# Low halves of the mixing projections' weights: the negated high half plus an accumulating transfer, in place of a subtraction

## The chip, the core and the metric

The kernel runs on one core of a Trainium2 chip. The metric is device time in microseconds (us) of one execution, smaller is better. Five engines work beside each other, each through its own instructions in order, tied together by semaphores: PE (TensorE, matmuls), DVE (VectorE), ACT (ScalarE), POOL (GpSimd) and SP (SyncE, which here only issues transfers). A queue of a transfer belongs to the engine that issues it; the data is moved by 16 DMA engines.

## The reference, cut to what matters

One encoder layer over 512 tokens of width 1024, all in float32:

```python
h = h + 0.5 * swiglu(rms_norm(h, ffn1_norm[l]), ...)
u = rms_norm(h, mix_norm[l]) @ w_in[l]            # 1024 -> q 512 | k 128 | v 128 | pool channels 512
q, k, v, pc = jnp.split(u, ...)
a = window_attention(rope(q), rope(k), v, sink_logits[l])
p = multiscale_pool(pc, pool_w[l], pool_scale[l])
h = h + jnp.concatenate([a, p], axis=-1) @ w_out[l]
h = h + 0.5 * swiglu(rms_norm(h, ffn2_norm[l]), ...)
return rms_norm(h, final_norm)
```

## The kernel before

**Precision.** Each large product is made of three matmuls in the format fp32r. An operand is split in a high half (a rounded copy) and a low half (the operand less its high half); `mm3` (L113) adds high by high, high by low and low by high in one PSUM bank. For activations the halves are called `xh`, `xl`, `yh`, `yl` and so on. For weights they are `wh` and `wl`, and in a projection of this kernel L114 is `wh` by `yh`, L115 `wh` by `yl`, and L116 `wl` by `yh`. So the third matmul of the first step of a weight half is the first that needs `wl`.

**Weight stream.** All weights come through one stream. A unit is 1 MB (128 x 2048), loaded by SP into one of two `raw` buffers; `split_next` (L78) takes one half of a unit (128 x 1024) at a time: ACT copies it to `wh` (L97), and DVE, or for a few halves POOL, subtracts `raw - wh` into `wl` (L98). There are four `wh` and four `wl` buffers, and `weights` (L103) splits up to two halves ahead of the one in use. A `raw` buffer is loaded anew when all that read it are done, and `wh` and `wl` are written anew when PE is done with them.

**The mixing part.** `w_in` is five units, ten halves of 24 matmuls each, in this order: k, v (woven into each other), pool channel group 3, query 0, group 2, queries 1, 2, 3, groups 1 and 0. I count them as first to tenth half. `w_out` is four units, eight halves. In before, POOL subtracts the first, second, fourth and sixth half of `w_in` and the first, fourth and seventh of `w_out` (the tables `WIN_POOL`, `WOUT_POOL`), and DVE the others.

**Work around it.** After the pool channel group 3 the sums of the norm are made (`norm_sums`) and spread (`norm_spread`, L198 on PE, L199 on ACT). Then DVE turns each product into what attention needs: for a query the rotation (`rope`, L357 to L360, with `u` as result), a scaled copy by ACT (L390), and the low half (L391) into `qq`. `pool_means` (L410) scales a group on DVE into `uu` (L418), sums windows on POOL (L425, L431, `dd` at L434), and goes back to DVE (L437) and on. Scores are two matmuls (L518, L519), a masked sum on DVE (L520) and an exponential on ACT (L523); POOL divides (L530); transposes (L547), copies (L551, L552) and products (L562, L563) follow. The order in which each engine takes its instructions is fixed when the program is built, by a scheduler that goes by estimated times, so an edit can move instructions that it doesn't touch.

Of the kernel before, what the change touches and what calls it, by code (L numbers as in the profile page):

```python
# [8 lines left out]
F32 = mybir.dt.float32  # L9
F32R = mybir.dt.float32r  # L10
AF = mybir.ActivationFunctionType
ALU = mybir.AluOpType
# [14 lines left out]
AFTER = 11  # L27
EARLY = 12
LAG = 4
WIN_POOL = (0, 1, 3, 5)  # L30
WOUT_POOL = (0, 3, 6)
POOL_W = (2, 4, 8, 16)
PAD = 8

# [2 lines left out]
def encoder_layer(ctx: ExitStack, tc: tile.TileContext, xT, w1h, w1gu, w1d, win, wout, w2h, w2gu, w2d,  # L37
                  gains, gfin, sinks, poolw, pscale, cosT, sinT, edges, out):
    nc = tc.nc
# [15 lines left out]
    units = [(w1h, i) for i in range(KD // 2)] + [(w1gu, i) for i in range(NF - F0)]  # L55
# [7 lines left out]
    def load(i, between=None):  # L63
        src, j = units[i]
        n = src.shape[-1] // 2
        if i in early:
            return early.pop(i)
        raw = wts.tile([P, 2048], F32, name="raw", tag="raw", bufs=2)
        if i == 0:
            for q in range(4):  # L70
                between(q)
                queue = nc.sync if q else nc.scalar
                queue.dma_start(raw[:, q * n // 2:(q + 1) * n // 2], src[j][:, q * n // 2:(q + 1) * n // 2])
        else:
            nc.sync.dma_start(raw[:, :2 * n], src[j])
        return raw, n

    def split_next():  # L78

        i, half = stream["asked"] // 2, stream["asked"] % 2  # L80
        if i == len(units):
            return
        if half == 0 and i:
            stream["raw"] = load(i)
        raw, n = stream["raw"]
        src = raw[:, half * n:(half + 1) * n]
        spare = stream.get("spare")
        if spare:
            wh, wl = spare.pop(0)
        else:  # L90
            wh = wts.tile([P, 1024], F32R, name="wh", tag="wh", bufs=4)[:, :n]
            wl = wts.tile([P, 1024], F32R, name="wl", tag="wl", bufs=4)[:, :n]
        m = n // 2 if stream["asked"] == 0 else n
        on_pool = WIN_POOL if units[i][0] is win else WOUT_POOL if units[i][0] is wout else ()
        sub = nc.gpsimd if 2 * units[i][1] + half in on_pool else nc.vector
        for c in range(0, n, m):
            nc.scalar.copy(wh[:, c:c + m], src[:, c:c + m])  # L97
            sub.tensor_tensor(wl[:, c:c + m], src[:, c:c + m], wh[:, c:c + m].bitcast(F32),  # L98
                              op=ALU.subtract)
        stream["asked"] += 1  # L100
        stream["ready"].append((wh, wl))

    def weights(ahead=2):  # L103
        while len(stream["ready"]) <= ahead and stream["asked"] < 2 * len(units):
            split_next()
        return stream["ready"].pop(0)
# [686 lines left out]
```

## Time and profile before

| What | us |
|---|---|
| median of 3 runs (lowest, highest) | 891.06 (889.69, 891.23) |
| the profiled execution's own time | 891.37 |
| its span | 889.6 |
| PE busy in the span | 872.2 (98%) |
| DVE busy | 408.4 (46%) |
| ACT busy | 309.9 (35%) |
| POOL busy | 311.8 (35%) |
| mean granted TensorE clock | 0.994 |

The span is the profiled stretch from the first instruction to the last; some 1.8 us lie around it. Matmul ends are modelled, so the distance from one matmul's start to the next one's (0.23 us for 512 columns at full clock) tells more than a duration of 0.39 us. The page's chain of work that ended last goes through PE for 92% and through DVE for 4%.

### The profile page before, as it was taken

The numbers are of one execution on the slowest core, as the hardware profiler recorded it, in microseconds if no ns is written. First come the engines' busy times: TensorE is split into PE (matmuls) and PEld (weight loads), VectorE is DVE, ScalarE is ACT, GpSimd is POOL, SyncE is SP. The second block draws the span as 40 slices with busy tenths as digits, with TensorE's granted clock in tenths as the row PEclk, the third lists the DMA queues.
The fourth block names the chain that finished last, engine by engine and source line by source line (L and its number), as shares of the span: only waits on it lengthen the run. The fifth ranks groups of instructions, "written<-read, shape, count | busy, mean of one in ns | idle before, by whom it ended". The sixth has DMA issues, their size and how long they took to land.

```text
span 889.6 us, 9675 instructions
## 1 busy us (share of the span) xinstructions
PE 872.2 (98%) x3918; PEld 719.3 (81%) x3918; DVE 408.4 (46%) x516; ACT 309.9 (35%) x454; POOL 311.8 (35%) x255
## 2 busy tenths in 40 slices
PE   8999999999999999999789999999999999999996
PEld 7888888888888888887668888888888888888885
DVE  6444444444432221669887643444444444322225
ACT  7353222333321111543666532533323322211223
POOL 5186444444420001855542220763444444200004
PEclk9999999999999999999999999999999999999998
DMA  6422222222222222221211123122222222332202
GB/s 237 156 81 95 95 97 98 102 106 101 104 102 95 95 95 95 84 95 50 97 44 36 61 93 125 66 95 95 94 95 95 95 94 95 127 104 104 105 11 94
DMA packets 14683, 84.79 MB, mean 95 GB/s; under 512 B 1824, under 2 KB 2352, under 8 KB 5808
## 3 DMA queue, kind: packets, MB, share of 16 engines
q1 hardware_dynamic: 13104, 81.60, 25.8%
q10 hardware_dynamic: 1440, 2.57, 0.9%
q8 instruction: 30, 0.49, 0.2%
q14 instruction: 13, 0.11, 0.0%
q0 software_dynamic: 96, 0.02, 0.0%
HBM read 82.08 MB, written 2.10 MB: 95 GB/s over the span
## 4 chain that ended last, share of the span: by engine, by line
PE 92%; DVE 4%; ACT 1%; POOL 1%; issue 1%; DMA 0%; DVEq 0%; POOLq 0%; ACTq 0%
PE ps L114 29%; PE ps L115 29%; PE ps L116 29%; DVE qq L391 1%; PE ps L547 1%; DVE wl L98 1%; PE ps L563 1%; PE ps L562 1%; DVE rtmp L359 1%; DMA small<-in_gains 0%; PE ps L655 0%; DVE u L360 0%; PE ps L226 0%; PE ps L228 0%; PE ps L198 0%
## 5 line engine op out<-in xcount | busy, mean ns | idle before, releaser
L98 DVE TENSOR_TENSOR wl<-raw,wh 128x1024 fp32r<-128x1024 f32 (+2 forms) x146 | 215.6, 1478 | 206.2 <-ACT wh L97 197.7
L97 ACT CAST wh<-raw 128x1024 fp32r<-128x1024 f32 (+2 forms) x153 | 156.3, 1024 | 415.1 <-PE ps L115 339.3
L114 PE MATMUL ps<-zh,wh 128*128 128x512 f32 x346 | 135.5, 392 | 0.0
L115 PE MATMUL ps<-zl,wh 128*128 128x512 f32 x346 | 135.1, 390 | 0.0
L116 PE MATMUL ps<-xh,wl 128*128 128x512 f32 x346 | 135.0, 391 | 0.0
L114 PE MATMUL ps<-xh,wh 128*128 128x512 f32 x346 | 134.8, 390 | 0.0
L116 PE MATMUL ps<-zh,wl 128*128 128x512 f32 x346 | 134.8, 390 | 0.0
L115 PE MATMUL ps<-xl,wh 128*128 128x512 f32 x346 | 134.6, 389 | 0.0
L208 POOL TENSOR_TENSOR t<-t,t 128x512 f32<-128x512 f32 x44 | 77.7, 1769 | 146.0 <-ACT t L207 146.0
L210 POOL TENSOR_TENSOR t<-t,rstd 128x512 f32<-128x512 f32 x44 | 61.2, 1394 | 99.3 <-DVE t L209 99.3
L209 DVE TENSOR_TENSOR t<-ps,t 128x512 f32<-128x512 f32 x44 | 30.4, 691 | 120.2 <-PE ps L116 108.2
L114 PEld LDWEIGHTS ps<-xh,wh 128*128 128x128 f32 x346 | 64.9, 188 | 13.9 <-ACT wh L97 0.2
L116 PEld LDWEIGHTS ps<-zh,wl 128*128 128x128 f32 x346 | 64.9, 188 | 13.9 <-issue 0.2
L116 PEld LDWEIGHTS ps<-xh,wl 128*128 128x128 f32 x346 | 64.9, 188 | 14.0 <-issue 0.2
L115 PEld LDWEIGHTS ps<-zl,wh 128*128 128x128 f32 x346 | 65.0, 188 | 13.4 <-issue 0.2
L115 PEld LDWEIGHTS ps<-xl,wh 128*128 128x128 f32 x346 | 65.0, 188 | 13.4
L114 PEld LDWEIGHTS ps<-zh,wh 128*128 128x128 f32 x346 | 65.0, 188 | 13.2
L206 DVE TENSOR_TENSOR t<-ps,rstd 128x512 f32<-128x512 f32 x44 | 30.2, 691 | 92.3 <-PE ps L116 75.9
L114 PE MATMUL ps<-a1h,wh 128*128 128x512 f32 x176 | 68.5, 389 | 0.0
L115 PE MATMUL ps<-a1l,wh 128*128 128x512 f32 x176 | 68.5, 389 | 0.0
L116 PE MATMUL ps<-a1h,wl 128*128 128x512 f32 x176 | 68.5, 389 | 0.0
L98 POOL TENSOR_TENSOR wl<-raw,wh 128x1024 fp32r<-128x1024 f32 x7 | 16.8, 2396 | 117.3 <-ACT wh L97 114.3
(189 smaller groups left out, 1270.2 us busy)
## 6 DMA issues: line engine op xcount, KB each, us to landing
raw<-in_w1gu SPq DMA_DIRECT2D x19, 1024.0 KB, 4.7
raw<-in_w2gu SPq DMA_DIRECT2D x19, 1024.0 KB, 4.7
raw<-in_w1d SPq DMA_DIRECT2D x11, 1024.0 KB, 4.7
raw<-in_w2d SPq DMA_DIRECT2D x11, 1024.0 KB, 4.8
raw<-in_win SPq DMA_DIRECT2D x5, 1024.0 KB, 4.7
raw<-in_wout SPq DMA_DIRECT2D x4, 1024.0 KB, 4.8
raw<-in_w2h SPq DMA_DIRECT2D x4, 768.0 KB, 4.2
raw<-in_w1h SPq DMA_DIRECT2D x3, 768.0 KB, 4.3
```

The costliest lines, as they stand in the source:

```text
L97: nc.scalar.copy(wh[:, c:c + m], src[:, c:c + m])
L98: sub.tensor_tensor(wl[:, c:c + m], src[:, c:c + m], wh[:, c:c + m].bitcast(F32), op=ALU.subtract)
L114: nc.tensor.matmul(ps, lhsT=ah, rhs=bh, start=start, stop=False)
L115: nc.tensor.matmul(ps, lhsT=ah, rhs=bl, start=False, stop=False)
L116: nc.tensor.matmul(ps, lhsT=al, rhs=bh, start=False, stop=stop)
L206: nc.vector.tensor_tensor(t1, pg, rstd, op=ALU.mult)
L208: nc.gpsimd.tensor_tensor(t2, t2, t1, op=ALU.mult)
L209: nc.vector.tensor_tensor(t1, pu, t2, op=ALU.mult)
L210: nc.gpsimd.tensor_tensor(t1, t1, rstd, op=ALU.mult)
L359: nc.vector.tensor_tensor(rot, rot, sr, op=ALU.mult)
L391: nc.vector.scalar_tensor_tensor(t[o, :], u[r, :], -HD ** -0.5, t[r, :].bitcast(F32), op0=ALU.mult, op1=ALU.subtract)
L547: nc.tensor.transpose(ps[:, i * P:(i + 1) * P], sc[g][0][:, i, (b - lo) * P:(b - lo + 1) * P], ident)
```

## The change

For halves of `w_in` and `w_out` the subtraction is gone. Of `w_in`, ACT writes the negated `wh` into `wl`, after its copy. Of `w_out`, POOL does that. Then a transfer issued by POOL adds `raw` to what stands in `wl` (`accum_op=ALU.add`, from SBUF to SBUF, 512 KB). All other weights are split as before. The two tables are gone.

```diff
-WIN_POOL = (0, 1, 3, 5)
-WOUT_POOL = (0, 3, 6)
...
-        on_pool = WIN_POOL if units[i][0] is win else WOUT_POOL if units[i][0] is wout else ()
-        sub = nc.gpsimd if 2 * units[i][1] + half in on_pool else nc.vector
         for c in range(0, n, m):
             nc.scalar.copy(wh[:, c:c + m], src[:, c:c + m])
-            sub.tensor_tensor(wl[:, c:c + m], src[:, c:c + m], wh[:, c:c + m].bitcast(F32),
-                              op=ALU.subtract)
+            if units[i][0] is win or units[i][0] is wout:
+
+                if units[i][0] is win:
+                    nc.scalar.activation(wl[:, c:c + m], wh[:, c:c + m].bitcast(F32), AF.Copy, scale=-1.0)
+                else:
+                    nc.gpsimd.tensor_scalar(wl[:, c:c + m], wh[:, c:c + m].bitcast(F32), -1.0, 1.0,
+                                            op0=ALU.mult, op1=ALU.mult)
+                nc.gpsimd.dma_start(wl[:, c:c + m], src[:, c:c + m], accum_op=ALU.add)
+            else:
+                nc.vector.tensor_tensor(wl[:, c:c + m], src[:, c:c + m], wh[:, c:c + m].bitcast(F32),
+                                        op=ALU.subtract)
```

Lines behind the edit have numbers five higher in the changed kernel (L425 is L430 there, L437 is L442). The rows below are what stands in an engine's order, without times.

POOL, about where PE comes to the third half of `w_in`, first before, then with the change (`uu` are pool channels, `pwh` and `pwl` the pool weights' halves, `s` window sums):

```order
L416 MEMSET uu 128x8
L417 MEMSET uu 128x8
L98 TENSOR_TENSOR wl<-raw,wh 128x1024
L329 CAST pwh<-pw 128x512
L330 TENSOR_TENSOR pwl<-pw,pwh 128x512
L98 TENSOR_TENSOR wl<-raw,wh 128x1024
L425 TENSOR_TENSOR s_2582<-uu 128x527
```

```order
L421 MEMSET uu 128x8
L422 MEMSET uu 128x8
L101 DMA wl<-raw 128x1024
L334 CAST pwh<-pw 128x512
L101 DMA wl<-raw 128x1024
L335 TENSOR_TENSOR pwl<-pw,pwh 128x512
L101 DMA wl<-raw 128x1024 x4
L430 TENSOR_TENSOR s_2588<-uu 128x527
```

The first DMA here is that of the third half, which DVE subtracted before; it stands behind everything that POOL does ahead of the fourth half's subtraction before.

ACT in the same place, first before, then with the change (`edge` and `pw` are small loads issued by ACT, `rstd` is the spread norm, L190 and L195 the square root of the sums):

```order
L324 DMA edge<-in_edges 128x30
L326 DMA pw<-in_poolw 128x512
L97 CAST wh<-raw 128x1024 x4
L190 ACT_TABLE_LOAD
L190 ACTIVATE small<-ps,small 128x4
L199 COPY rstd<-ps 128x512
```

```order
L329 DMA edge<-in_edges 128x30
L331 DMA pw<-in_poolw 128x512
L97 ACTIVATE wl<-wh 128x1024
L93 CAST wh<-raw 128x1024
L97 ACTIVATE wl<-wh 128x1024
L93 CAST wh<-raw 128x1024 x2
L97 ACTIVATE wl<-wh 128x1024 x2
L195 ACT_TABLE_LOAD
L195 ACTIVATE small<-ps,small 128x4
L93 CAST wh<-raw 128x1024
L97 ACTIVATE wl<-wh 128x1024
L204 COPY rstd<-ps 128x512
```

The third half's negation stands behind the small load of `pw`, and the seventh half's copy and negation stand now ahead of the copy of `rstd`.

POOL at the windows of pool channel group 1, before and with the change (L425 and L430 sum windows, L431 and L436 correct the edges, `dd` goes to DVE):

```order
L417 MEMSET uu 128x8
L98 TENSOR_TENSOR wl<-raw,wh 128x1024
L425 TENSOR_TENSOR s_2825<-uu 128x527
L425 TENSOR_TENSOR s_2835<-s_2825 128x525
L431 TENSOR_TENSOR s_2835<-s_2835,edge 128x2 x2
L434 TENSOR_TENSOR dd<-s_2835 128x512
```

```order
L99 TENSOR_SCALAR wl<-wh 128x1024
L101 DMA wl<-raw 128x1024
L430 TENSOR_TENSOR s_2836<-uu 128x527
L99 TENSOR_SCALAR wl<-wh 128x1024
L430 TENSOR_TENSOR s_2847<-s_2836 128x525
L101 DMA wl<-raw 128x1024
L436 TENSOR_TENSOR s_2847<-s_2847,edge 128x2 x2
L439 TENSOR_TENSOR dd<-s_2847 128x512
```

Between `uu` and `dd` POOL has now a negation and a DMA of `w_out` as well.

DVE at the last query and the first scores, before and with the change (L520 and L525, shown as ISA, are the masked sum of a score):

```order
L357 STREAM_SHUFFLE rtmp<-ps 128x512
L358 TENSOR_TENSOR u<-ps,cr 128x512
L391 SCALAR_TENSOR_TENSOR qq<-u,qq 64x512 x2
L359 TENSOR_TENSOR rtmp<-rtmp,sr 128x512
L98 TENSOR_TENSOR wl<-raw,wh 128x1024
L360 TENSOR_TENSOR u<-u,rtmp 128x512
L418 TENSOR_TENSOR uu<-ps,rstd 128x512
L98 TENSOR_TENSOR wl<-raw,wh 128x1024
L391 SCALAR_TENSOR_TENSOR qq<-u,qq 64x512 x2
L520 ISA sc,st<-ps,mask,small 128x256
L520 ISA st 128x1
L437 SCALAR_TENSOR_TENSOR dd<-dd,uu 128x512
```

```order
L362 STREAM_SHUFFLE rtmp<-ps 128x512
L363 TENSOR_TENSOR u<-ps,cr 128x512
L364 TENSOR_TENSOR rtmp<-rtmp,sr 128x512
L365 TENSOR_TENSOR u<-u,rtmp 128x512
L396 SCALAR_TENSOR_TENSOR qq<-u,qq 64x512 x2
L423 TENSOR_TENSOR uu<-ps,rstd 128x512
L525 ISA sc,st<-ps,mask,small 128x256
L525 ISA st 128x1
L525 ISA sc,st<-ps,mask,small 128x256
L525 ISA st 128x1
L442 SCALAR_TENSOR_TENSOR dd<-dd,uu 128x512
```

The subtractions are gone, each `qq` pair follows its own `u` at once, and `uu` stands behind the last pair. On PE one thing moved: L198, which spreads the norm, stands three matmuls earlier.

## Rows read from the trace of the kernel before

**Rows 1.** The page's busy times: busy us, share of the span, instructions.

```profile
PE 872.2 (98%) x3918; PEld 719.3 (81%) x3918; DVE 408.4 (46%) x516; ACT 309.9 (35%) x454; POOL 311.8 (35%) x255
```

**Rows 2.** Stretches: us; PE, PEld, DVE, ACT, POOL busy; clock, DMA share, GB/s.

```profile
390.70:431.80 41.10, 37.69 (x181) 30.98 (x180) 40.49 (x54) 16.02 (x23) 21.22 (x24) 0.99 0.23 78
...
456.00:518.00 62.00, 61.39 (x307) 50.53 (x306) 46.30 (x89) 37.94 (x77) 19.17 (x25) 1.00 0.11 39
```

**Rows 3.** PE's waits, whole span: us in total, times, longest us.

```profile
PE ps L518 <- DVE qq L391: 2.5, 1, 2.5
...
PE ps L116 <- DVE wl L98: 0.9, 2, 0.6
```

**Rows 4.** DVE in order of time: start us, us, line, operation, idle time before.

```profile
401.93 2.00 DVE L98 TENSOR_TENSOR wl<-raw,wh 128x1024 fp32r<-128x1024 f32 x1
...
426.99 0.68 DVE L418 TENSOR_TENSOR uu<-ps,rstd 128x512 f32<-128x512 f32 x1
427.59 1.21 DVE L98 TENSOR_TENSOR wl<-raw,wh 128x1024 fp32r<-128x1024 f32 x1
428.83 2.91 DVE L391 SCALAR_TENSOR_TENSOR qq<-u,qq 64x512 fp32r<-64x512 f32 x2
...
433.10 0.69 DVE L437 SCALAR_TENSOR_TENSOR dd<-dd,uu 128x512 f32<-128x512 f32 x1 [0.83 <-POOL dd L434]
```

**Rows 5.** PE in order of time, just after its 2.5 us wait.

```profile
430.90 0.62 PE L114 MATMUL ps<-yh,wh 128*128 128x512 f32 x1
431.31 0.63 PE L115 MATMUL ps<-yl,wh 128*128 128x512 f32 x1
...
433.24 0.41 PE L519 MATMUL ps<-kl,qq 128*128 128x256 f32 x1
```

**Rows 6.** ACT in order of time.

```profile
357.12 1.05 ACT L97 CAST wh<-raw 128x1024 fp32r<-128x1024 f32 x1 [4.38 <-PE ps L115]
...
374.65 0.34 ACTq L326 DMA_DIRECT2D pw<-in_poolw  x1
375.03 1.05 ACT L97 CAST wh<-raw 128x1024 fp32r<-128x1024 f32 x1 [3.53 <-POOL acc L171]
...
390.67 0.59 ACT L199 COPY rstd<-ps 128x512 f32<-128x512 f32 x1 [3.72 <-PE ps L198]
...
421.77 1.29 ACT L390 ACTIVATE qq<-u 64x512 fp32r<-64x512 f32 x2 [3.45 <-DVE u L360]
```

**Rows 7.** POOL in order of time.

```profile
376.94 2.40 POOL L98 TENSOR_TENSOR wl<-raw,wh 128x1024 fp32r<-128x1024 f32 x1
379.28 0.62 POOL L329 CAST pwh<-pw 128x512 fp32r<-128x512 f32 x1
...
427.75 1.97 POOL L425 TENSOR_TENSOR s<-uu 128x527 f32<-128x527 f32 x1 [14.63 <-DVE uu L418]
...
432.02 1.04 POOL L434 TENSOR_TENSOR dd<-s 128x512 f32<-128x512 f32 x1
```

**Rows 8.** PE in order of time, at the start of the third half.

```profile
379.14 0.39 PE L115 MATMUL ps<-yl,wh 128*128 128x512 f32 x1
379.36 0.39 PE L116 MATMUL ps<-yh,wl 128*128 128x512 f32 x1
```

**Rows 9.** DMA issues: tiles, queue, count, KB each, median us from issue to landing.

```profile
raw<-in_win SPq DMA_DIRECT2D x5, 1024.0 KB, 4.7
...
out<-hT ACTq DMA_DIRECT2D x4, 256.0 KB, 2.0
...
gf<-in_gfin ACTq DMA_DIRECT2D x1, 512.0 KB, 3.8
...
small<-in_gains POOLq DMA_DIRECT2D x1, 12.0 KB, 4.4
```

**Rows 10.** Groups of POOL instructions: count, busy us, mean ns, idle before.

```profile
L129 POOL DMA_DIRECT2D small<-in_gains x1 | 0.7, 749 | 0.8 <-POOLq L782 0.8
...
L530 POOL TENSOR_SCALAR sc<-sc,st 128x384 f32<-128x384 f32 x16 | 9.6, 625 | 0.7 <-DVE st L528 0.7
```

## The prediction

> **What bounds the kernel now.** I read the busy times first: PE is busy for 98% of the span and no other engine for half of it [rows 1]. So nothing is gained outside PE's waits. The table by stretches then says where these are. From 456 to 518 us, where `w_out` is used, PE is busy for 61.39 of 62.00 us; from 390.7 to 431.8 us it lacks 3.4 us, and there DVE is busy for 40.49 of 41.10 [rows 2]. The list of PE's waits names that engine: 2.5 us in one wait for the last query's `qq`, and 0.9 us in two waits for `wl`, which are subtractions that stood too far back in DVE's order [rows 3]. DVE's own rows show five subtractions in this stretch, the first of 2.00 us, stretched beside POOL, the other four like the last, 1.21 to 1.22: 6.9 us together [rows 4].
>
> After the wait of 2.5 us PE also ran slowly: 0.41 us from one 512-column matmul to the next [rows 5], against 0.22 earlier [rows 8]. That is the lower of TensorE's two levels (1.2 and 2.4 GHz). It lasts from the wait's end to about 433.4 [rows 5], some 3 us, so half of it, about 1.4 us, is a second price of that wait.
>
> **DVE's relief.** With the change DVE loses the five subtractions, 6.9 us [rows 4]. Not all of that shows. Before, a subtraction and parts of the next rotation stood between a query's `u` and its `qq`, and ACT's copy ran meanwhile; now the `qq` pair follows at once and DVE waits for the first of ACT's two copies, half of 1.29 us [rows 6], for three queries: 2.0 us. So the last `qq` pair, which ended at 431.7 [rows 4], ends at 431.7 - 6.9 + 2.0 = 426.8. The pair took 2.91 us beside POOL's first window sum, which was stretched too, to 1.97 [rows 4, 7]; now `uu` stands behind the pair and they no longer overlap. A pair alone is twice `uu`'s 0.68 [rows 4], so 1.5 us more are saved: 425.3, and `uu` is done at 426.0, against 427.7 before.
>
> **What is late next.** DVE's third score waits in order behind `dd` of pool group 1 (L437), which before waited 0.83 us for POOL and began at 433.10 [rows 4]. POOL's way from `uu` to `dd` was 427.67 to 433.06, 5.4 us [rows 4, 7]. It loses the overlap, at most 0.9 us, as I estimate from 1.97 against `dd`'s 1.04 for nearly as many elements. It gains a negation of 1024 columns and the issue of a transfer. No row has that negation: it lies between 0.63, for 384 columns with the same kind of instruction [rows 10], and the 2.40 of the subtraction [rows 7]; I take 1.4, nearer to the 384 columns scaled up (1.67) than to two-operand work. An issue on POOL is 0.75 [rows 10]. So `dd` is there at 426.0 + 5.4 - 0.9 + 1.4 + 0.75 = 432.7, which is 0.4 earlier than before. L198 stands three matmuls earlier, at 0.22 each [rows 8] 0.7 us, and DVE's chain starts with the norm. That makes **1.0 us of gain** in place of the 3.4 plus 1.4 that PE's waits promised: POOL ends last where DVE did, and everything behind the first scores moves with it.
>
> **The new wait.** The third half of `w_in` is needed first at 379.36 [rows 8]. Before, DVE subtracted it soon after ACT's copy. Now ACT negates it only after the load of `pw`, which is itself kept back, by POOL's norm sums, until 374.65 [rows 6]; its copy-sized negation, 1.05 [rows 6], ends at 376.1. POOL comes to the transfer after its memsets, where the fourth half's subtraction began: 376.94 [rows 7]. Issue 0.75, then the flight.
>
> The flight has no row. The nearest are 2.0 us for 256 KB, 3.8 for 512 KB and 4.7 for 1 MB, all issued by ACT or SP, and 4.4 for 12 KB issued by POOL [rows 9]. The last is that queue, though in the busy first microseconds. To it I add what 512 KB more cost between the two larger ones, 0.9: **5.3 us**. Ends: 2.0, and twice 4.7, so 9.4, for a transfer that reads both its source and its target. With 5.3 it lands at 376.94 + 0.75 + 5.3 = 383.0, and **PE waits 3.6 us** at its first L116. With 2.0 it waits 0.3, with 9.4 it waits 7.7.
>
> By the Trainium skill, page "DMA: Bandwidth & Descriptors", section "Anatomy of one DMA", a transfer issued by GpSimd takes about 2.0 us and its bytes at 436 GB/s. "Collectives: The Full Stack", section "The bandwidth ceiling", adds that the transfer's add costs no time by itself but needs two source reads. For 1 MB read that is an estimate of 4.4 us, a wait of 2.7 and a sum 0.9 lower than mine. The rows have no transfer that adds, so none agrees or disagrees yet.
>
> A wait of 3.6 us is longer than that of 2.5, after which the clock fell. I charge the same **1.4 us** again; ends 0 and 2.
>
> **The rest.** The second half is copied from 357.12, so negated by 359.2 [rows 6]; PE needs it 48 matmuls before the third, at 0.22 each [rows 8] about 368.8, so its flight could be 8 us, and that of the first half, copied a half earlier, more. ACT's further negations, 1.05 each [rows 6], go beside a PE that needs those halves later. One is hidden with little to spare: the seventh half's load must now wait for the fourth half's transfer, issued at 378.3 behind the `pwh` copy [rows 7]. That lands at 384.4, the load of 4.7 [rows 9] ends at 389.1 and the copy and negation on ACT at 391.2, ahead of the copy of `rstd`, which moves from 390.67 [rows 6] to 393.6 with the wait. A longer flight moves both alike, so these 2.4 us stay; if the load is slowed by more than that, each further us delays the norm and DVE. In `w_out` each half has a copy, 1.4, 0.75 and 5.3 to make, 8.5 us, while PE works on three others of 24 matmuls, 16 us at 0.22 each [rows 8]; no wait comes to the busy stretch of [rows 2].
>
> **Sum.** 3.6 + 1.4 - 1.0 = +4.0 us. The profiled execution took 891.37, its span 889.6; the median of the runs is 891.06, 0.3 lower. So the changed kernel's span would be 893.6 and its median **895.1**.
>
> **The rivals.**
>
> *Faster: the flight is short.* If it lands by 379.4, in 1.7 us or less, PE doesn't wait. At 2.0 us it waits 0.3, which left the clock alone elsewhere (the two waits of 0.9 in all). Then DVE's relief stands alone: -1.0 at least, and -4.9 if POOL's negation and issue are so short that PE's 2.5 us wait and its slow stretch vanish. That is 886.2 to 890. For it speaks the 2.0 row; against it the 4.4 on POOL's own queue [rows 9]. It decides with a flight below 2.5 us, or a `dd` some 3 us earlier than I have it.
>
> *No change: the sum cancels.* With 3.8 us of flight, as for 512 KB [rows 9], the wait is 2.1; if the clock then stays up, 2.1 - 1.0 is +1.1, so 892.2, and with 2 us more of relief 890.2.
>
> *Much slower: adding halves the rate or worse.* At 9.4 us the wait is 7.7; with 1.4 for the clock and 1.0 of gain that is +8.1, so 899. Each us of flight beyond is at least one more, since the second half then waits too: a flight of 12 us goes to 902 and past it. For it speaks that nothing in these rows reads, adds and writes; against it that 1 MB flies in 4.7 [rows 9].
>
> That the change doesn't do what it says I can leave out: DVE's order has no subtraction of these halves, and POOL's has eighteen transfers.
>
> **How the numbers follow.** The forecast, a wait of 2.5 to 5 us behind the third half, has 0.46: 892.9 to 898. Much slower 0.17, no change 0.16, faster 0.21. A measurement of this kernel can tell 0.2%, 1.8 us, from no change. Slower by more than that is the forecast and the much slower case, 0.63; within it 0.16; faster 0.21. A range that leaves out about a tenth on each side goes from 888 to 903.
>
> **What would show it.** Right: a wait of PE at L121 (the old L116) near 379 us that ends with a transfer into `wl`, of 2.5 to 5 us; matmuls at 0.41 us behind it; DVE idle before L442 for over 2 us with POOL's `dd` as its releaser; no wait for `wl` later. The DMA table should have 18 issues of 512 KB on POOL with 4 to 7 us to landing. Wrong: landings below 3 us, or no wait at 379; then the sign turns. A `dd` that comes much earlier than 432 us plus the wait would say that I overpriced POOL's negation and issue; waits at the fifth to tenth half, that I underpriced the flight beside a busy DVE.

## The result, and the profile after

| | before | after |
|---|---|---|
| median, us (runs) | 891.14 (4) | 895.51 (4) |
| lowest, highest, us | 889.69, 891.25 | 895.35, 896.01 |
| profiled execution, us | 891.37 | 895.57 |
| its span, us | 889.6 | 893.8 |
| mean granted TensorE clock | 0.994 | 0.992 |

The changed kernel takes 1.0054 times as long, with a 95% interval of 1.0036 to 1.0071: 4.4 us slower. The page's busy times answer to [rows 1]; DVE lost 11 us of work, ACT gained 10, and PE is where it was.

```profile
PE 872.9 (98%) x3918; PEld 720.9 (81%) x3918; DVE 397.2 (44%) x505; ACT 320.2 (36%) x464; POOL 313.4 (35%) x274
```

The table by stretches (us; PE, PEld, DVE, ACT, POOL busy with their instructions; clock, DMA share, GB/s), of after, answers to [rows 2]:

```profile
368.00:390.70 22.70, 21.65 (x100) 17.53 (x98) 5.70 (x15) 11.86 (x15) 13.29 (x21) 1.00 0.74 175
390.70:431.80 41.10, 40.36 (x197) 33.34 (x195) 31.94 (x53) 23.18 (x32) 23.91 (x30) 1.00 0.62 156
431.80:456.00 24.20, 14.84 (x63) 12.65 (x64) 18.29 (x44) 14.18 (x40) 15.87 (x29) 0.79 0.48 131
456.00:518.00 62.00, 61.30 (x307) 50.00 (x306) 43.29 (x88) 38.94 (x79) 21.50 (x30) 1.00 0.28 73
```

From 390.7 to 431.8 us PE is now busy for 40.36 us, 2.7 more than before: the relief of DVE came. From 431.8 to 456 it is busy for 14.84 of 24.20, at a clock of 0.79. The same stretch of before, which [rows 2] leave out, is this:

```profile
431.80:456.00 24.20, 20.19 (x94) 15.75 (x92) 18.06 (x53) 19.16 (x49) 14.87 (x25) 0.88 0.11 44
```

So the time is lost there, in a stretch in which the prediction had only a gain. PE's waits in after (us in total, times, longest) say in which two places; they answer to [rows 3]:

```profile
PE ps L568 <- DVE pl L557: 4.9, 1, 4.9
PE ps L523 <- DVE st L525: 4.9, 2, 4.5
...
PE ps L121 <- DMA wl<-raw: 1.0, 1, 1.0
```

The wait for `qq` and those for DVE's `wl` are gone. The third half's new wait, the main term of the prediction, is the small one. PE in order of time shows it, and the matmuls behind it at 0.23 us, so the clock didn't fall:

```profile
380.50 0.50 PE L121 MATMUL ps<-yh,wl 128*128 128x512 f32 x1 [1.05 <-DMA wl<-raw]
380.84 0.39 PE L119 MATMUL ps<-yh,wh 128*128 128x512 f32 x1
381.07 0.40 PE L120 MATMUL ps<-yl,wh 128*128 128x512 f32 x1
```

Where do the two large waits come from? DVE in order of time (start, duration, operation, idle time before it and its releaser):

```profile
394.41 0.69 DVE L485 TENSOR_TENSOR cr<-cr,rstd 128x512 f32<-128x512 f32 x1 [2.38 <-ACT rstd L204]
...
427.06 1.40 DVE L396 SCALAR_TENSOR_TENSOR qq<-u,qq 64x512 fp32r<-64x512 f32 x2 [0.70 <-ACT qq L395]
428.50 0.69 DVE L423 TENSOR_TENSOR uu<-ps,rstd 128x512 f32<-128x512 f32 x1
434.73 0.69 DVE L442 SCALAR_TENSOR_TENSOR dd<-dd,uu 128x512 f32<-128x512 f32 x1 [4.73 <-POOL dd L439]
...
446.89 4.47 DVE L442 SCALAR_TENSOR_TENSOR dd<-dd,uu 128x512 f32<-128x512 f32 x1 [1.13 <-POOL dd L439]
451.28 0.68 DVE L557 TENSOR_TENSOR pl<-ps,ph 128x512 fp32r<-128x512 f32 x1
```

DVE starts the rotations late, behind ACT's copy of `rstd`, and is late from there to `dd` of group 1, which it reads at 434.73 (433.10 in [rows 4]). Then, at the last pool group, the same instruction that takes 0.69 us everywhere else takes 4.47, and `pl`, for which PE waits, stands behind it. POOL beside it:

```profile
444.05 0.88 POOL L101 DMA_DIRECT2D wl<-raw  x1
444.67 0.62 POOL L436 TENSOR_TENSOR s<-s,edge 128x1 f32<-128x1 f32 x2
444.98 0.86 POOL L535 TENSOR_SCALAR sc<-sc,st 128x384 f32<-128x384 f32 x1
445.54 1.31 POOL L439 TENSOR_TENSOR dd<-s 128x512 f32<-128x512 f32 x1
446.56 1.93 POOL L535 TENSOR_SCALAR sc<-sc,st 128x384 f32<-128x384 f32 x3
448.21 0.41 POOL L516 COPY sc<-small 128x4 f32<-128x4 f32 x1
448.38 2.43 POOL L535 TENSOR_SCALAR sc<-sc,st 128x384 f32<-128x384 f32 x4
```

One of the eight divisions of block 1 (L535) now stands ahead of `dd` and seven behind it. POOL's rows overlap here: the next division counts as started at 446.56, 0.29 us before `dd` is done (445.54 + 1.31 = 446.85). DVE comes to L442 at 446.89 and is through at 451.36, half a us after the seven are done (448.38 + 2.43 = 450.81). I call this L442 the held instruction. In before all eight stood behind `dd`, the first counts as started only 0.03 us before `dd` was done, and DVE got in 0.06 us after that start:

```profile
445.87 0.69 DVE L437 SCALAR_TENSOR_TENSOR dd<-dd,uu 128x512 f32<-128x512 f32 x1 [2.67 <-POOL dd L434]
446.48 0.17 DVE L528 RECIPROCAL st<-st 128x4 f32<-128x4 f32 x1
446.57 0.66 DVE L552 TENSOR_TENSOR pl<-ps,ph 128x512 fp32r<-128x512 f32 x1
```
```profile
444.80 1.04 POOL L434 TENSOR_TENSOR dd<-s 128x512 f32<-128x512 f32 x1
445.81 5.06 POOL L530 TENSOR_SCALAR sc<-sc,st 128x384 f32<-128x384 f32 x8
```

L442 reads `dd` and `uu`, both in SBUF; the `pl` row of before, which reads PSUM and SBUF, ran at 0.66 beside the same divisions. The Trainium skill, page "SBUF — State Buffer", section "SBUF: two separate sides", says that a DVE instruction with two inputs in SBUF and a GpSimd instruction that reads SBUF exclude each other, and that whichever starts first keeps the other out for a whole instruction. That they exclude each other agrees with the traces. How long does not: the 4.47 us are a run of seven divisions and a copy, not one instruction. Nor does the order of the starts decide it by these rows: in before too the division counts as started first, and there it was the division that was held (its own part of the 5.06 us is 1.12, the seven behind it have a mean of 0.56). The measurements decide.

The late `rstd` is seen on ACT:

```profile
391.70 1.05 ACT L93 CAST wh<-raw 128x1024 fp32r<-128x1024 f32 x1 [4.82 <-DMA raw<-in_win]
392.79 1.06 ACT L97 ACTIVATE wl<-wh 128x1024 fp32r<-128x1024 f32 x1
393.75 0.57 ACT L204 COPY rstd<-ps 128x512 f32<-128x512 f32 x1
```

The copy of `rstd` came at 390.67 in [rows 6], and now 3.1 us later, behind the seventh half's copy and negation. That half's load, issued at 383.18, took 8.5 us to land, where such a load has a median of 4.7 in [rows 9]; these are the transfers under way between 383 and 384 us:

```profile
raw<-in_win SPq DMA_DIRECT2D x1, 1024.0 KB, 8.5
wl<-raw POOLq DMA_DIRECT2D x1, 512.0 KB, 9.1
```

### The profile page after: what moved, and what is told of

It reads as the page before. It is cut to its first block, busy times and chain, and to the rows that moved or that the text cites. A ratio compares the mean times of both kernels' runs of the same rounds, so it can differ in the third digit from the quotient of the medians.

```text
span 893.8 us, 9718 instructions
## 1 busy us (share of the span) xinstructions
PE 872.9 (98%) x3918; PEld 720.9 (81%) x3918; DVE 397.2 (44%) x505; ACT 320.2 (36%) x464; POOL 313.4 (35%) x274
## 4 chain that ended last, share of the span: by engine, by line
PE 88%; POOL 4%; DVE 3%; DMA 2%; issue 2%; ACT 1%; DVEq 0%; ACTq 0%; POOLq 0%; SPq 0%
PE ps L119 28%; PE ps L120 28%; PE ps L121 28%; POOL s L430 1%; DMA raw<-in_win 1%; PE ps L552 1%; DVE yl L165 1%; PE ps L568 1%; DMA wl<-raw 1%; PE ps L567 1%; POOL wl L101 1%; DVE h L306 1%; DMA small<-in_gains 0%; POOL dd L439 0%; PE ps L660 0%
## 5 line engine op out<-in xcount | busy, mean ns | idle before, releaser
L93 ACT CAST wh<-raw 128x1024 fp32r<-128x1024 f32 (+2 forms) x153 | 156.3, 1024 | 406.9 <-PE ps L120 329.0
L103 DVE TENSOR_TENSOR wl<-raw,wh 128x1024 fp32r<-128x1024 f32 (+2 forms) x135 | 201.3, 1494 | 193.3 <-ACT wh L93 192.1
L121 PE MATMUL ps<-xh,wl 128*128 128x512 f32 x346 | 134.9, 390 | 0.0
L121 PE MATMUL ps<-zh,wl 128*128 128x512 f32 x346 | 134.8, 390 | 0.0
L121 PEld LDWEIGHTS ps<-zh,wl 128*128 128x128 f32 x346 | 64.9, 188 | 13.8 <-issue 0.2
L121 PEld LDWEIGHTS ps<-xh,wl 128*128 128x128 f32 x346 | 64.9, 188 | 13.8 <-issue 0.2
L121 PE MATMUL ps<-a1h,wl 128*128 128x512 f32 x176 | 68.5, 389 | 0.0
L101 POOL DMA_DIRECT2D wl<-raw x18 | 15.7, 872 | 124.3 <-ACT wl L97 120.0
```

Of the source, the lines that this page charges most:

```text
L101: nc.gpsimd.dma_start(wl[:, c:c + m], src[:, c:c + m], accum_op=ALU.add)
L103: nc.vector.tensor_tensor(wl[:, c:c + m], src[:, c:c + m], wh[:, c:c + m].bitcast(F32), op=ALU.subtract)
L121: nc.tensor.matmul(ps, lhsT=al, rhs=bh, start=False, stop=stop)
```

## The experiments

Two theories stood at first. **W_IN**: the loss sits where `w_in` is split, in the third half's wait and the late `rstd`. **W_OUT**: it sits where `w_out` is split, in POOL's negations and the held instruction. All runs were timed beside the kernel before, at 891.2 us. The diffs are against the changed kernel and cut to the main lines. What stands ahead of this stage moves by up to 1.9 us from trace to trace (e7 below), so moments of two traces can be compared only that closely.

### e1_win_only: the change for `w_in` alone

```diff
-            if units[i][0] is win or units[i][0] is wout:
+            if units[i][0] is win:
...
+                sub = nc.gpsimd if units[i][0] is wout and 2 * units[i][1] + half in (0, 3, 6) else nc.vector
```

> Only w_in's halves are made by negation (ACT) and adding transfer; w_out's are subtracted as before (three on POOL, five on DVE). Theory W_IN (the loss sits where w_in is split: PE's wait of 1.05 us for the third half, and the copy of rstd on ACT that came 3.1 us later behind the seventh half's late copy and negation): the loss stays, 894 to 896, with that wait and DVE's idle time of some 2.4 us ahead of the rotations. Theory W_OUT (the loss sits where w_out is split: POOL's negations and issues between the pool channels and dd, and one normalisation of POOL that slipped ahead of the last dd, so that DVE's L442 took 4.47 us in place of 0.69): 890 to 892, the two-operand subtraction of dd at 0.7 us and PE's waits near 431 to 436 us at 2 to 4 us.

Measured: 896.01 us, 1.0058 (1.0046 to 1.0071). `dd` of group 1 is read at 436.33, 3.2 us later than before, and reading that of the last group takes 0.69:

```profile
436.33 0.69 DVE L438 SCALAR_TENSOR_TENSOR dd<-dd,uu 128x512 f32<-128x512 f32 x1 [3.63 <-POOL dd L435]
...
450.50 0.69 DVE L438 SCALAR_TENSOR_TENSOR dd<-dd,uu 128x512 f32<-128x512 f32 x1 [2.60 <-POOL dd L435]
```

So W_IN is right, as far as it goes: this part alone costs the whole loss, without the held instruction.

### e2_wout_only: the change for `w_out` alone

```diff
-            if units[i][0] is win or units[i][0] is wout:
+            if units[i][0] is wout:
...
+                sub = nc.gpsimd if units[i][0] is win and 2 * units[i][1] + half in (0, 1, 3, 5) else nc.vector
```

> Only w_out's halves are made by negation (POOL) and adding transfer; w_in's are subtracted as before (four on POOL, six on DVE). Theory W_IN: no wait at the third half, rstd copied at 390.7 us as before, and DVE rid of w_out's subtractions: 888.5 to 891. Theory W_OUT: POOL's order at the last dd is the same as in the whole change, one normalisation ahead of it and seven behind: the DVE instruction that reads dd takes 4 to 5 us again, PE waits some 5 us for pl, 894 to 896.

Measured: 895.65 us, 1.0052 (1.0040 to 1.0064). There is no wait at the third half, but the held instruction is there to the hundredth, and PE's wait for `pl` is 5.0 us:

```profile
446.76 4.47 DVE L439 SCALAR_TENSOR_TENSOR dd<-dd,uu 128x512 f32<-128x512 f32 x1 [1.10 <-POOL dd L436]
```

W_OUT is right too. Each part alone costs as much as both together, so neither theory is the whole, and the parts' losses don't add.

### e3_neg_on_act: all negations on ACT

```diff
-                if units[i][0] is win:
-                    nc.scalar.activation(...)
-                else:
-                    nc.gpsimd.tensor_scalar(...)
+                nc.scalar.activation(wl[:, c:c + m], wh[:, c:c + m].bitcast(F32), AF.Copy, scale=-1.0)
```

> The whole change, but w_out's eight negations stand on ACT too; POOL only issues. POOL then has dd of the last group directly ahead of its eight normalisations, as in the kernel before, and the dd of group 1 loses a negation of 1.04 us on its way. Theory W_IN: the wait of 1.05 us and the late rstd stay, and so does the time: 894 to 896.5. Theory W_OUT: L437 (the dd less the token) takes 0.7 us, the wait of PE for pl falls from 4.9 to under 2 us, dd of group 1 is read a us earlier: 890 to 892.

Measured: 889.34 us, 0.9985 (0.9976 to 0.9993), below either range. DVE reads the last `dd` in 0.69 us, 0.05 after POOL's first division started, as before:

```profile
445.50 0.69 DVE L437 SCALAR_TENSOR_TENSOR dd<-dd,uu 128x512 f32<-128x512 f32 x1 [0.53 <-POOL dd L434]
```

The third half's wait (1.1 us) and the late `rstd` are still there: it comes at 394.95, in a trace in which PE also comes to the third half 1.4 us later than in after (381.87 against 380.50). So the relief of DVE outweighs them here. They are not free: e5 shows what they cost.

### e4_no_transfer: no transfers

```diff
-                nc.gpsimd.dma_start(wl[:, c:c + m], src[:, c:c + m], accum_op=ALU.add)
```

> The whole change without its eighteen transfers: wl is left as the negated high half, so the low part of the mixing weights is wrong. Both theories: no wait at the third half, the seventh half's load starts some 3 us earlier and rstd is copied at about 391 us, and POOL has dd directly ahead of the normalisations: 888 to 890.5. This is what the relief of DVE is worth when the transfers and their issues cost nothing. If it is not below 890.5 the loss is in the negations themselves, on ACT or POOL.

Measured: 886.03 us, 0.9939 (0.9927 to 0.9951), below the expected range. `rstd` is copied at 390.53. This is what the change is worth when its transfers and their issues cost nothing, 5.2 us below before; the negations alone are not where the loss is. POOL's order changed too: no division stands ahead of the last `dd`.

### e6_forced2: the last `dd` ahead of the divisions

```diff
                 nc.gpsimd.tensor_tensor(box["dd"], cur[:, o:o + S], cur[:, o + 1:o + 1 + S], op=ALU.add)
+                if gi == 0:
+                    box["one"] = cut(70, 1)
+                    nc.gpsimd.tensor_scalar(box["one"], box["dd"][:, 0:1], 0.0, 1.0, op0=ALU.mult, op1=ALU.add)
+                    one.append(box["one"])
...
-                    nc.gpsimd.tensor_scalar(sc[:, j, :w], sc[:, j, :w], st[:, 0, j:j + 1], 1.0,
-                                            op0=ALU.mult, op1=ALU.mult)
+                    nc.gpsimd.tensor_scalar(sc[:, j, :w], sc[:, j, :w], st[:, 0, j:j + 1],
+                                            one[0] if (n, g) == (1, 0) else 1.0, op0=ALU.mult, op1=ALU.mult)
```

> The whole change; POOL's first division of block 1 is made to depend on dd of the last pool group (through a constant 1 that POOL writes behind dd, 128x1), so that dd stands ahead of all eight divisions again. POOL keeps its negations and issues. Theory BLOCK (DVE's read of that dd is held by POOL's run of divisions because one of them already ran when dd came, and this 4.47 us instruction is most of the loss): L443 to L448's dd instruction takes 0.7 us, PE's wait for pl falls from 4.9 to under 2 us, 891 to 892.5. Rival (any run of divisions behind dd holds DVE, or the 4.47 us only hide another wait): the instruction still takes over 3 us or another wait of 3 us or more takes its place, 894.5 to 896.

Measured: 891.16 us, 1.0002 (0.9994 to 1.0011): 4.35 us of the 4.4 are gone. DVE, then PE's waits:

```profile
446.97 0.69 DVE L447 SCALAR_TENSOR_TENSOR dd<-dd,uu 128x512 f32<-128x512 f32 x1 [2.33 <-POOL small L443]
```
```profile
PE ps L528 <- DVE st L530: 4.9, 2, 4.5
...
PE ps L573 <- DVE pl L562: 0.8, 1, 0.8
```

DVE starts the read at the same time as in after (446.89), but 0.08 us ahead of the first division (447.05), and is done at once. The wait for `pl` falls from 4.9 to 0.8; the other one is untouched. POOL still issues a transfer just ahead of these steps, so the issue alone doesn't hold DVE.

### e8_div_on_act: block 1's divisions on ACT

```diff
+                    if n == 1:
+                        nc.scalar.activation(sc[:, j, :w], sc[:, j, :w], AF.Copy, scale=st[:, 0, j:j + 1])
+                        continue
```

> The whole change; the eight divisions of block 1 (128x384) are made by ACT, so that POOL has none near the last dd. Theory BLOCK: the last dd is read in 0.7 us, PE's wait for pl is under 2 us, 891 to 893 (ACT's eight scalings of some 0.5 us may cost part of the gain). Rival: the time stays at 895 to 896, with a wait of PE for ph or pl that ACT now ends.

Measured: 892.33 us, 1.0009 (1.0001 to 1.0017); the `dd` is read in 0.69 us, and PE waits 1.2 us for ACT's `ph` instead. A second way to the same end: the held instruction was the loss, and what it waited for was POOL's divisions.

### e7_rstd_dve: `rstd` copied by DVE

```diff
-        norm_spread(spread)
+        norm_spread(spread, nc.vector.tensor_copy)
```

> The whole change; only the copy of the mixing norm's rstd is made by DVE, which waits for it anyway, and no longer by ACT behind the seventh half. Theory LOAD (the late rstd costs DVE some 2.4 us): DVE begins the rotations at some 391 to 392 us in place of 394.4, the last qq pair and the dd of group 1 come about 2 us earlier, PE's wait of 4.5 us near 436 us falls to 2 or 3; 892 to 894, since the 4.5 us instruction of the last dd stays. Theory BLOCK alone: DVE is earlier but PE only waits longer at the held instruction, 895 to 896.

Measured: 894.21 us, 1.0032 (1.0020 to 1.0044), just above the expected 892 to 894: 1.3 us less than after. In this trace everything ahead of the stage stands 1.9 us later than in after (ACT's negation of the third half begins at 376.00, there at 374.12), so the copy at 393.22 is 2.4 us earlier than ACT's at 393.75 was. PE's wait of 4.5 falls to 2.8, and the 4.47 us instruction stays:

```profile
393.22 0.69 DVE L204 COPY rstd<-ps 128x512 f32<-128x512 f32 x1 [2.48 <-PE ps L203]
...
446.18 4.47 DVE L442 SCALAR_TENSOR_TENSOR dd<-dd,uu 128x512 f32<-128x512 f32 x1 [1.13 <-POOL dd L439]
```

### e9_both: e6 and e7 at once

The edits are those of e6_forced2 and e7_rstd_dve.

> The whole change with both mendings of before at once: the last dd ahead of POOL's divisions (as e6_forced2) and rstd copied by DVE (as e7_rstd_dve). If the held instruction (worth 4.35 us there) and the late rstd (worth 1.3 us there) are separate losses, they add: 895.51 - 4.35 - 1.3 = 889.9, so 889 to 890.5. If the one only uncovers the other, as when PE waits at the next place for the same chain, it stays at e6_forced2's 891.2 (890.8 to 891.6).

Measured: 888.35 us, 0.9974 (0.9963 to 0.9986), 0.65 below the expected range. The late `rstd` is worth 2.8 us once the held instruction is gone (891.16 to 888.35), and 1.3 with it. So neither alternative holds as it stands: the late `rstd` is a loss of its own, but the two don't add, since the held instruction hid half of it. Both `dd` come earlier than before:

```profile
432.08 0.69 DVE L447 SCALAR_TENSOR_TENSOR dd<-dd,uu 128x512 f32<-128x512 f32 x1 [4.73 <-POOL dd L440]
...
444.11 0.69 DVE L447 SCALAR_TENSOR_TENSOR dd<-dd,uu 128x512 f32<-128x512 f32 x1 [2.35 <-POOL small L443]
```

### e10_late_win: only the last six halves of `w_in`

```diff
-            if units[i][0] is win or units[i][0] is wout:
+            asked = 2 * units[i][1] + half
+            if units[i][0] is win and asked >= 4:
...
+                sub = nc.gpsimd if units[i][0] is win and asked in (0, 1, 3) or units[i][0] is wout and asked in (0, 3, 6) else nc.vector
```

> As e1_win_only (only w_in is changed; 896.0 us), but the first four halves of w_in are subtracted as in the kernel before, so only its last six are negated and added. Theory LOAD (e1_win_only loses by the late load of the seventh half alone, since DVE with w_out's subtractions has no room for 3 us of delay): rstd at about 391 us, no wait of PE at the third half, dd of group 1 read 3 us earlier than in e1_win_only, 889 to 891.5. Rival (transfers beside the loads or POOL's issues cost the time whichever halves they serve): 893.5 to 896.

Measured: 891.10 us, 0.9997 (0.9988 to 1.0006), 4.9 below e1_win_only. So in `w_in` it was the first four halves that cost the time, and by e4 their transfers, not their negations: the third half's is waited for, and the fourth's keeps the seventh's load waiting. The other six are free, and as long as `w_out` is subtracted they bring nothing.

### e5_early_sub: early halves subtracted, all negations on ACT

```diff
-            if units[i][0] is win or units[i][0] is wout:
+            asked = 2 * units[i][1] + half
+            if units[i][0] is wout or (units[i][0] is win and asked >= 4):
+                nc.scalar.activation(wl[:, c:c + m], wh[:, c:c + m].bitcast(F32), AF.Copy, scale=-1.0)
...
+                sub = nc.gpsimd if units[i][0] is win and asked in (0, 1, 3) else nc.vector
```

> As e3_neg_on_act (every negation on ACT), but the first four halves of w_in are subtracted as in the kernel before (first, second and fourth on POOL, third on DVE). Theory LOAD (the seventh half's load waits until the fourth half's adding transfer has landed, and its cast and negation then hold back ACT's copy of rstd, so that all of DVE starts 3 us late; and PE waits 1.1 us for the third half): no wait at the third half, the load starts some 3 us earlier, rstd is copied at about 391 us, and the time falls by 2 to 3 us against e3_neg_on_act's 889.3: 886.5 to 887.5. Rival (what e3_neg_on_act still lacks against the kernel without transfers lies in POOL's issues, at about 0.87 us each, and in the transfers beside other work): 888.5 to 890.

Measured: 884.68 us, 0.9929 (0.9917 to 0.9941), below what was expected and **faster than both kernels**: 6.6 us below before, 10.8 below after. Against e3_neg_on_act, which differs only in the first four halves, it is 4.7 us (2 to 3 were expected): so much the third half's wait and the late `rstd` cost there. ACT's copy of `rstd` waits for PE alone, and the stretch that lost the time has PE busy for 22.40 of 24.20:

```profile
390.89 0.59 ACT L201 COPY rstd<-ps 128x512 f32<-128x512 f32 x1 [2.74 <-PE ps L200]
```
```profile
431.80:456.00 24.20, 22.40 (x115) 17.93 (x116) 22.41 (x66) 23.27 (x61) 15.86 (x29) 0.93 0.26 71
```

## Why the prediction was right, and where it wasn't

The sign was right and the size was close (+4.0 forecast, +4.4 measured), but the sum came out through other terms than those it was made of, so the close number is luck. By the prediction's own signs its case did not come: the wait at L121 is below its 2.5 to 5 us, and no matmul behind it steps at 0.41.

- **The new wait, 3.6 us: 1.05 measured.** The place, the half and the releaser were right; the size was not. POOL came to the transfer at 376.02, not at 376.94, and the transfer landed some 4.4 us after its issue began, where 0.75 + 5.3 = 6.05 had been put. The value between the bounds was too far up: 4.4 is what the 12 KB transfer on POOL's own queue took [rows 9], and the 0.9 for more bytes on top was not there. Nor was the 0.75 to be added: the times of [rows 9] count from the issue, as 376.02 + 4.4 = 380.42 and PE's start at 380.50 show. The estimate by the Trainium skill's page "DMA: Bandwidth & Descriptors", section "Anatomy of one DMA", 4.4 us, was the better one if it is counted from the issue's start. The rows are POOL's issues for the third and the fourth half:

```profile
376.02 0.82 POOL L101 DMA_DIRECT2D wl<-raw  x1
...
377.51 0.85 POOL L101 DMA_DIRECT2D wl<-raw  x1
```

- **The clock, 1.4 us: nothing there.** After 1.05 us PE stepped at 0.23. The half clock came elsewhere: behind the wait of 4.5 us PE steps by 0.43 us, as at 439.34 and 439.77:

```profile
435.88 0.69 PE L523 MATMUL ps<-kk,qq 128*128 128x384 f32 x1 [4.51 <-DVE st L525]
...
439.34 0.63 PE L119 MATMUL ps<-yh,wh 128*128 128x512 f32 x1
439.77 0.63 PE L120 MATMUL ps<-yl,wh 128*128 128x512 f32 x1
```

- **"These 2.4 us stay": they did not.** This step failed. It let the load that follows the fourth half's transfer take its usual 4.7 us. That transfer, issued at 377.51, landed earlier than was put, the load was issued at 383.18, and then took 8.5 us beside two more adding transfers, with the DMA share at 0.90 from 383 to 392 us. The cover of 2.4 us, rightly named as thin, was gone, and 3.1 us of delay came to `rstd`, worth 1.3 us by e7 and 2.8 by e9. The copy at 393.75 is close to the 393.6 of the prediction, again by luck: there it waited for a late PE, here for ACT's own work. SP's issue, and the table by stretches for the flight:

```profile
383.18 8.70 SPq L73 DMA_DIRECT2D raw<-in_win  x2
```
```profile
383.00:392.00 9.00, 9.00 (x43) 7.20 (x42) 2.50 (x12) 0.90 (x3) 0.19 (x1) 1.00 0.90 226
```

- **DVE's relief, -1.0 us.** The rule was right (`qq` follows `u` at once, DVE waits for half of ACT's pair, 0.70 us, then for POOL's `dd`), but the value was too small. In e9, without the two mishaps, `dd` of group 1 is read at 432.08 with the wait of 1.05 still ahead of it, and the kernel is 2.8 us faster than before; so the relief is some 3.8 us, if that wait costs its own length. At `dd` itself it is 2.1 us (433.10 before, 432.08 - 1.05 here). Where the rest comes from was not tried; the clock from 431.8 to 456 us was 0.93 in e9 and 0.88 in before. POOL's way from `uu` to `dd` was overpriced: from 429.2 to 434.7 in after, 5.5 us, in place of 6.65. The negation took 1.05, not 1.4, and the issue runs partly beside the next instruction.
- **What the prediction had no term for: the held instruction, 4.35 us by e6.** It asked what is queued at `dd` of group 1 and didn't look at the last group, though POOL's order, one division ahead of `dd`, is fixed when the program is built. It also left out the stretch in which this lies: in before PE lacks 4.0 us from 431.8 to 456, more than the 3.4 of the stretch that it read. It had no price for a DVE instruction that meets a run on POOL, although two stretched rows, 2.00 us and 2.91 us beside POOL [rows 4], showed such meetings.
- **Right:** no wait for `wl` after the third half, none in `w_out`, whose stretch keeps PE busy for 61.30 of 62.00; the eighteen transfers on POOL with a median of 4.5 us; and DVE idle for 4.73 us ahead of L442 with POOL's `dd` as the releaser.

The measured terms give 1.05 (wait) + 4.35 (held, e6) + 2.8 (`rstd`, e9) - 3.8 (relief) = +4.4. This closes by construction and tests nothing: the first is the wait's length, and the last is what e9 leaves when the others are taken off; neither was measured by itself.

## What to carry to other kernels

An accumulating transfer takes work off an engine, but its target and its source stay taken until it lands: use it only for tiles that are needed late and whose source nobody waits to reload. When an edit lets a scheduler reorder an engine, read every place where a two-input DVE instruction meets a run of POOL's, not only the place that the edit is about. If a change saves work in a stretch and the time still goes up, split it by its parts first: here each part alone lost as much as both, and with the faults of both mended (e5) the same idea made the kernel 6.6 us faster than before.

## What the runs showed of the hardware

- The same DVE instruction with two SBUF inputs took 0.69 us where it came 0.05 or 0.06 us after POOL's run of divisions had started (before, e1, e3, e10), and 4.47 us where one division of the run was in POOL ahead of `dd` (after, e2, e7): it was kept out for the whole run. In the first four traces the division behind `dd` counts as started 0.02 or 0.03 us before `dd` is done, and is itself drawn out to 1.11 or 1.12 us; in the other three it counts as started 0.25 to 0.30 us before. Whether the division ahead does it by itself, or only together with the transfer that POOL issued before it, was not tried.
- An adding transfer of 512 KB from SBUF to SBUF took 4.4 to 9.1 us from the start of its issue to landing, with a median of 4.5, and held POOL for 0.87 us to issue; a load of 1 MB beside two of them took 8.5 (in e4, without the adding transfers, that load took 4.7):

```profile
wl<-raw POOLq DMA_DIRECT2D x18, 512.0 KB, 4.5
```
```profile
L101 POOL DMA_DIRECT2D wl<-raw x18 | 15.7, 872 | 124.3 <-ACT wl L97 120.0 <-PE ps L120 2.6 <-POOL wl L99 1.2
...
L99 POOL TENSOR_SCALAR wl<-wh 128x1024 fp32r<-128x1024 f32 x8 | 8.4, 1046 | 27.9 <-ACT wh L93 27.8
```

- POOL's negation of 1024 columns, one input, took 1.05 us, as long as ACT's (1.06), where its subtraction with two inputs took 2.40 [rows 7].
